# A weight sum's low part moved from VectorE to ScalarE and an accumulating DMA in an FFN up projection

## The chip, the cores and the metric

The kernel runs on one core of one Trainium2 chip, as one program with one launch. The metric is the time of the execution on the device in microseconds (us). Engines are named as in the profile: PE is TensorE's matmul, PEld its weight load, DVE is VectorE, ACT is ScalarE, POOL is GpSimd, SP is SyncE, which here only issues DMAs.

## The reference

The program is a two-layer trunk in float32 over 512 positions and 1024 channels. Each layer normalises, mixes the tokens (layer 0 by pooling and a short convolution, layer 1 by gated linear attention), adds the result to `x`, and then runs a feed-forward block, which is where the change lies:

```python
D_MODEL = 1024; SEQ = 512; DEPTH = 2; D_FF = 2816

def conv_ffn(h, w_up, conv_w, conv_b, w_down):
    u, v = jnp.split(h @ w_up, 2, axis=-1)
    u = causal_dwconv(u, conv_w, conv_b)
    return (jax.nn.gelu(u, approximate=False) * v) @ w_down

def reference(...):
    for l in range(DEPTH):
        ...
        x = x + conv_ffn(rmsnorm(x, ffn_norm[l]), ffn_w_up[l], ffn_conv_w[l], ffn_conv_b[l], ffn_w_down[l])
    return rmsnorm(x, final_norm)
```

`h @ w_up` is 512 by 1024 times 1024 by 5632 in each layer.

## The kernel before

**Two parts of every operand.** Each float32 operand is split into a high part (a copy rounded to the matmul's float32r format, written by ACT) and a low part (operand minus high part, written by DVE). A product is then three passes: weight high by data high, weight high by data low, weight low by data high.

**Pairs.** The 5632 columns of `w_up` are taken as 22 pairs, numbered here from 0 as in the code (`seven(j, base)`); a pair holds 128 columns of `v` and 128 of `u`. A pair is done with seven block products instead of eight (p1 to p7), after Strassen and Winograd. Each is three passes of four matmuls of 128x256 and is one `UNIT` (1.364 us) of the plan, so a pair is 7 units, 9.55 us. The products p1 and p2 use the left half `a1` of the pair's weights, p6 uses `s2`, p5 and p7 use the sum `s31`, p3 and p4 use the last combination `a2`. They are not done in one block: p4 and p3 of a pair come 9 and 11 units after its start, between the products of the next pair (`PE_AT`). So from a pair's start ("base") PE does p1, p2, p4 of the pair before, p6, p3 of the pair before, p5, p7. In pair 0 the order is p1, p2, p3, p6, p5 (`PE_AT_FIRST`), and the products p2 and p3 there run the weight's low pass before the data's low pass (`low_last`).

**The weights of a pair** (`seven_weights`). SP loads the block that both halves of `s31` share (`load_sum`, line 462, 512 KB into three rotating buffers). GpSimd adds the other two blocks of `w_up` onto it by an accumulating DMA (`add_sum`, line 466, 512 KB). SP loads the left half (`load_left`, line 470, 512 KB) and the right half (`load_right`, line 474, 256 KB) into three rotating `raw` buffers. ACT and DVE make high and low parts (lines 484 and 490) of `a1`, `s31`, `s2` and `a2`; DVE forms `s2` and `a2` (lines 495, 501). A high and a low part of 128x1024 lie in four rotating buffers each (`wsp`).

**The rest of a pair.** ACT copies partial results out of PSUM (`keep`, line 645, tiles `kk`, `k`, `k3`; line 679, `u`), DVE combines them (657, 660, 682), the convolution is one ACT and two DVE steps (356, 359), gelu is on ACT (627).

**The order of work.** Each step is recorded with a planned time (`at`), sorted by it, and issued in that order on PE, DVE and ACT (`run_plan`, `manual_schedule`), which so keep an order written out by hand. SP's and GpSimd's queues are ordered by the scheduler. Each engine and each queue works strictly in its order: what waits holds up all that stands behind it. In the plan the high part of `s31` is due at base - 2.7, its low part at base + 1.5. The `lead` argument gives pairs 0 to 5 a later `a2` (high at base + 2.2, low at + 4.4, instead of + 0.4 and + 3.3).

Of the kernel before, what the change touches and what calls it, by code (L numbers as in the profile page):

```python
# [10 lines left out]
AF = mybir.ActivationFunctionType  # L11
ALU = mybir.AluOpType
# [29 lines left out]
UNIT = 1.364  # L42
# [13 lines left out]
DOWN_K = (7, 7)  # L56
DOWN_AT = (0, 7)
NDOWN = 6

COLS = {}  # L60
_n = 0
# [12 lines left out]
def trunk_kernel(ctx, tc, xT, cols, w_ab, w_pool, w_abo, w_vg, w_qk, w_r, w_g2, w_go, w_up, w_dn, w_ds, outT):  # L74
    nc = tc.nc
    V, S, G, PE = nc.vector, nc.scalar, nc.gpsimd, nc.tensor
# [9 lines left out]
    def slot(dt=F32, name="s"):  # L86
        return big.tile([P, T], dt, tag="s", name=name)
# [14 lines left out]
    def half(name):  # L102
        return hp.tile([P, H], F32, tag="h", name=name)
# [15 lines left out]
    lead = []  # L119
# [53 lines left out]
    def f32(ap):  # L173
        return ap.bitcast(F32)
# [189 lines left out]
    def conv3(u, wname, bname, j, nj):  # L364
        tap = conv_steps(u, wname, bname, j, nj)
        return [tap(i) for i in range(3)][0]
# [63 lines left out]
    def at(t, fn):  # L430
        events.append((t, len(events), fn))
# [21 lines left out]
        at(t_high, lambda: steps[0]())  # L453
        at(t_low, lambda: steps[1]())

    def seven_weights(src, base, pool, sums, behind=False, lead=None, later=0.0):
        w = {}

        def load_sum():
            s31 = w["s31"] = stage[pool].tile([P, WBLK], F32, tag="sum", name="s31", bufs=sums)  # L460
            part = src[:, None, D : D + QUARTER].broadcast_to([P, 2, QUARTER])
            nc.sync.dma_start(s31.rearrange("p (a n) -> p a n", a=2), part)

        def add_sum():
            part = src.rearrange("p (a n) -> p a n", a=4)[:, 0:4:3, :]
            G.dma_start(w["s31"].rearrange("p (a n) -> p a n", a=2), part, accum_op=ALU.add)  # L466

        def load_left():
            w["raw", 0] = wp.tile([P, WBLK], F32, tag="raw", name="raw")
            nc.sync.dma_start(w["raw", 0], src[:, :D])  # L470

        def load_right():
            w["raw", 1] = wp.tile([P, WBLK], F32, tag="raw", name="raw")
            nc.sync.dma_start(w["raw", 1][:, QUARTER:], src[:, D + QUARTER :])

        def tiles(kind, wide):
            if wide:
                return wsp.tile([P, WPITCH], F32R, tag=kind, name=kind)[:, SKEW : SKEW + WBLK]
            tag, bufs = "s" + kind[0], 2 if pool == "up" else 1
            return stage[pool].tile([P, T + 64], F32R, tag=tag, name=tag, bufs=bufs)[:, SKEW : SKEW + T]  # L480

        def high(name, src, wide=True):
            h = tiles("hi", wide)
            S.activation(h, src(), AF.Copy)  # L484
            w[name] = (h, src)

        def low(name, wide=True):
            h, src = w[name]
            lo = tiles("lo", wide)
            V.tensor_tensor(lo, src(), f32(h), ALU.subtract)  # L490
            w[name] = (h, lo)

        def s2_sum():
            s2 = w["raw", 1][:, :QUARTER]
            V.scalar_tensor_tensor(
                s2, w["s31"][:, QUARTER:], -1.0, w["raw", 0][:, :QUARTER], ALU.mult, ALU.subtract
            )

        def s4_sum():
            s2 = w["raw", 1][:, :QUARTER]  # L500
            V.tensor_tensor(s2, w["raw", 0][:, QUARTER:], s2, ALU.subtract)

        def queued_sum():
            with tc.issue_after(loads[-1]):
                load_sum()

        at(base - 26.0, queued_sum if behind else load_sum)
        at(base - 20.0, add_sum)
        steps = (
            (lambda: high("a1", lambda: w["raw", 0])), (lambda: low("a1")), (lambda: high("s31p", lambda: w["s31"])),  # L510
            s2_sum, (lambda: high("s2", lambda: w["raw", 1][:, :QUARTER], False)), (lambda: low("s2", False)),
            s4_sum, (lambda: high("a2", lambda: w["raw", 1])), (lambda: low("s31p")), (lambda: low("a2")),
        )
        when = (-6.75, -4.35, -2.7, -2.4, -1.65, -0.95, -0.3, 1.55, 1.5, 3.3)
        if pool == "up":
            when = (*when[:7], *((2.2, 1.5, 4.4) if lead is not None else (0.4, 1.5, 3.3)))
        if pool == "gla":
            when = (*when[:7], 4.4, 1.5, 5.3)
        if lead is not None and lead < 2:
            when = ((-9.5, -7.6, 2.6, -8.3, -7.0, -6.0, -5.3, -4.5, 4.3, -2.6), (-3.9, -1.9, -1.2, -2.4, -1.65, -0.95, -0.3, 2.4, 1.5, 4.6))[lead]  # L520
        at(base - (18.0 if lead == 0 else 15.4), load_left)
        at(base - (13.0 if lead == 0 else 9.7), load_right)
        for n, (t, step) in enumerate(zip(when, steps)):
            at(base + t + ((0, 0, 1.2, 1.2, 0.6, 0.6)[lead or 0] if 3 <= n <= 6 else later if n == 0 else 0.0), step)

        return w
# [89 lines left out]
    def ffn(l, acc, mixed, finish, ahead, halves_last=False):  # L616
# [17 lines left out]

        def seven(j, base):
            b, q = {}, {}
            w = seven_weights(w_up[l, j], base, "up", 3, j <= 3, j if j < 6 else None, 0.8 if j in (6, 7) else 0.0)

            def product(*args):
                if not rhs:  # L640
                    rhs.update(operands(mixed))
                seven_product(w, b, rhs, *args)

            def keep(dst):
                S.activation(dst, b["x"][:, :H], AF.Copy)  # L645

            def keep_p1():
                q["k"] = slot(name="kk")
                keep(q["k"][:, lo_t])

            def keep_p7():
                q["k3"] = half("k3")
                keep(q["k3"])

            def u_high():
                q["u"] = slot(name="u")
                V.scalar_tensor_tensor(q["u"][:, hi_t], b["yz"][:, hi_t], -1.0, q["k3"], ALU.mult, ALU.subtract)

            def u_scaled():
                V.tensor_tensor(q["u"], q["u"], rs, ALU.mult)  # L660

            for name, out, first, ts in (
                ("p1", "x", True, lo_t), ("p2", "yz", True, lo_t), ("p6", "x", False, lo_t), ("p5", "yz", False, hi_t),
                ("p7", "x", False, lo_t), ("p4", "x", False, lo_t), ("p3", "yz", False, hi_t),
            ):
                apart = j in (0, NF - 1)
                if apart and name == "p3":
                    out, first = "w", True
                when = PE_AT_FIRST if j == 0 else PE_AT_LAST if j == NF - 1 else PE_AT
                t = base + when[name] * UNIT + (NORM if j == 0 and when[name] > 4 else 0.0)  # L670
                for i in range(3) if j == 0 and name == "p2" else (None,):
                    at(t + (i or 0) * UNIT / 3, lambda a=(name, out, first, ts, i, j == 0 and name in ("p2", "p3")): product(*a))
            late = UNIT + NORM if j == 0 else 0.0
            at(base + 1.45, keep_p1)
            at(base + (5.1 if j == 0 else 5.5 if j < 6 else 6.05), lambda: keep(q["k"][:, hi_t]))
            at(base + (9.0 if j == 2 else 8.25 if 2 < j < 6 else 9.55) + late, keep_p7)
            at(base + 9.95 + late, u_high)
            after = base + PAIR + (NORM + 1.6 if j == 0 else NORM + 0.5 if j == 1 else 0.0)
            at(after + 4.1, lambda: S.activation(q["u"][:, lo_t], b["x"][:, :H], AF.Copy, scale=-1.0))
            at(after + 4.5, u_scaled)  # L680
            conv_at(j, after, q)
            at(after + 10.4, lambda: V.tensor_tensor(q["k"], b["yz"], q["k"], ALU.add))
            if apart:
                hi_k = lambda: q["k"][:, hi_t]
                at(after + 10.5, lambda: V.tensor_tensor(hi_k(), b["w"][:, hi_t], hi_k(), ALU.add))
            at(after + 12.3, lambda: V.tensor_tensor(q["a"], q["k"], q["a"], ALU.mult))
# [3 lines left out]
        def split_m():  # L690
            j = len(mh)
            pool = stage["dn"] if j < NDOWN // 2 else big
            mh.append(pool.tile([P, T], F32R, tag="s", name="mh"))
# [52 lines left out]
        base = 5 * UNIT  # L746
# [3 lines left out]
        base -= PAIR  # L750
        at(base + 5.6, lambda: open_stage("dn", NDOWN))
        for t in (5.8, 6.6, 8.0, 10.3, 10.9, 11.5, 12.2, 14.5, 15.2, 16.4, 17.6, 18.3, 19.0, 20.6):
# [4 lines left out]
        o, late, ops = {}, {}, {}  # L757
# [75 lines left out]
        t = base + 9 * UNIT  # L833
# [70 lines left out]
    with tc.manual_schedule(engines=set(planned)):  # L904
        raw, hi, lo = lead[0]
# [75 lines left out]
    for j in range(4):  # L981
# [5 lines left out]
        a = conv3(c, "sc_w", "sc_b", j, 4)  # L987
# [281 lines left out]
    t = 0.0  # L1269
# [15 lines left out]
    first = True  # L1285
# [153 lines left out]
    late = t + 2.5  # L1439
# [152 lines left out]
```

## Time and profile before

| | |
|---|---|
| median of 3 runs | 1006.32 us (1005.56 to 1007.13) |
| profiled execution | 1006.93 us, of which the span is 1005.2 us |
| mean granted TensorE clock | 0.997 |
| PE busy | 994.8 us (99%) |
| DVE busy | 851.2 us (85%) |
| ACT busy | 615.8 us (61%) |
| POOL busy | 81.3 us (8%) |
| DMA, queue of SP (q1) | 117.46 MB, 37.8% of 16 engines' span |
| DMA, queue of GpSimd (q0) | 31.99 MB, 19.2% of 16 engines' span |

A row of the timeline gives start, length, engine, line, operation, what is written from what, the shape and a count; the brackets at its end give the idle time of the engine before it and what ended that. The kernel has stages: the input projection and mixer of layer 0 to about 140.6 us of the span, the up projection of layer 0 to 352, its down projection to about 475, the attention of layer 1, its up projection from about 668 to 879, and the last down projection. PE's busy share says little by itself, since matmuls are pipelined; what the kernel loses is seen where the starts of its groups of four matmuls lie further apart than elsewhere.

### The profile page before, as it was taken

The page shows a single profiled execution, that of the slowest core. Times are in us where ns is not written, and L with a number is a line of the kernel's source. Part 1 is how long each engine was busy: PE and PEld are TensorE (multiplying, and loading weights), DVE is VectorE, ACT ScalarE, POOL GpSimd, SP SyncE. Part 2 cuts the span into 40 slices and gives each one's busy share as a digit, 9 for nine tenths or more (in the row PEclk, how much of TensorE's full clock was granted, in tenths as well). Part 3 has the DMA queues.
Part 4 walks back from the last instruction along what each step waited for, and adds up shares of the span by engine and source line. Part 5 has one row for each costly group of instructions (what it writes and reads, how often), then busy time and mean ns, then how long its engine had stood idle before and what let it go on. Part 6 is the DMA issues. An engine that isn't in the chain of part 4 may idle for free.

```text
span 1005.2 us, 17757 instructions
## 1 busy us (share of the span) xinstructions
PE 994.8 (99%) x7070; PEld 927.9 (92%) x7070; DVE 851.2 (85%) x1241; ACT 615.8 (61%) x959; POOL 81.3 (8%) x105
## 2 busy tenths in 40 slices
PE   9999999999999999999999999999999999999996
PEld 7888889999999988899999998889999999988896
DVE  7886689999999997768768788889999999997775
ACT  6442467666766764445785677667766666754451
POOL 0000111111101000002000000111101101000000
PEclk9999999999999999999999999999999999999998
DMA  6523757787687454527326122676788777454522
GB/s 224 156 97 105 181 123 185 193 210 191 190 208 181 129 134 132 140 85 198 108 76 145 53 67 93 185 171 165 213 207 194 195 202 188 127 128 142 129 86 84
DMA packets 64083, 151.22 MB, mean 150 GB/s; under 512 B 5408, under 2 KB 8352, under 8 KB 64000
## 3 DMA queue, kind: packets, MB, share of 16 engines
q1 hardware_dynamic: 46640, 117.46, 37.8%
q0 software_dynamic: 16672, 31.99, 19.2%
q8 instruction: 55, 0.90, 0.3%
q10 hardware_dynamic: 688, 0.65, 0.2%
q14 instruction: 28, 0.23, 0.1%
HBM read 145.35 MB, written 2.10 MB: 147 GB/s over the span
## 4 chain that ended last, share of the span: by engine, by line
PE 91%; DVE 4%; DMA 2%; ACT 1%; issue 1%; DVEq 0%; ACTq 0%
PE stx L538 27%; PE styz L538 16%; PE dn L268 15%; PE r L1323 4%; PE abo L268 4%; PE go L268 4%; PE pc L268 2%; PE dn L538 2%; PE px L268 2%; PE pb L268 2%; DMA raw<-in_w_up 2%; PE stz L538 2%; PE vg L1111 1%; PE vg L1113 1%; PE vg L1112 1%; PE pu L268 1%
## 5 line engine op out<-in xcount | busy, mean ns | idle before, releaser
L490 DVE TENSOR_TENSOR lo<-raw,hi 128x1024 fp32r<-128x1024 f32 x112 | 136.7, 1221 | 14.1 <-ACT hi L484 13.8
L484 ACT ACTIVATE hi<-raw 128x1024 fp32r<-128x1024 f32 x112 | 117.8, 1057 | 33.2 <-DMA raw<-in_w_up 12.8
L227 DVE TENSOR_TENSOR lo<-raw,hi 128x1024 fp32r<-128x1024 f32 (+3 forms) x79 | 91.1, 1155 | 18.2 <-ACT hi L223 17.7
L466 POOL DMA_DIRECT2D s<-in_w_up x44 | 53.1, 1206 | 530.1 <-ACT yh L177 97.3
L223 ACT ACTIVATE hi<-raw 128x1024 fp32r<-128x1024 f32 (+3 forms) x79 | 78.7, 997 | 13.2 <-DMA raw<-in_w_ab 4.7
L359 DVE SCALAR_TENSOR_TENSOR cacc<-u,colt,cacc 128x511 f32<-128x511 f32 x96 | 71.5, 745 | 3.9 <-ACT cacc L356 3.8
L356 ACT ACTIVATE cacc<-u,colt 128x512 f32<-128x512 f32 x48 | 39.2, 817 | 49.5 <-DVE u L660 39.9
L490 DVE TENSOR_TENSOR lo<-s,hi 128x1024 fp32r<-128x1024 f32 x56 | 68.2, 1217 | 0.0
L538 PE MATMUL stx<-th,hi 128*128 128x256 f32 x384 | 59.4, 277 | 0.3 <-ACT kk L645 0.3
L484 ACT ACTIVATE hi<-s 128x1024 fp32r<-128x1024 f32 x56 | 59.0, 1053 | 0.7
L538 PE MATMUL stx<-th,lo 128*128 128x256 f32 x384 | 59.1, 276 | 0.0
L538 PE MATMUL stx<-tl,hi 128*128 128x256 f32 x384 | 59.1, 276 | 0.0
L538 PE MATMUL styz<-xl,hi 128*128 128x256 f32 x368 | 57.2, 277 | 0.3
L538 PE MATMUL styz<-xh,hi 128*128 128x256 f32 x368 | 56.9, 277 | 0.0
L538 PE MATMUL styz<-xh,lo 128*128 128x256 f32 x368 | 56.7, 276 | 0.0
L268 PE MATMUL dn<-mh,hi 128*128 128x512 f32 (+1 forms) x238 | 56.5, 377 | 0.0
L268 PE MATMUL dn<-mh,lo 128*128 128x512 f32 (+1 forms) x238 | 56.4, 376 | 0.0
L268 PE MATMUL dn<-ml,hi 128*128 128x512 f32 (+1 forms) x238 | 56.4, 376 | 0.0
L538 PEld LDWEIGHTS stx<-th,hi 128*128 128x128 f32 x384 | 50.7, 188 | 0.7 <-ACT kk L645 0.7
L538 PEld LDWEIGHTS stx<-tl,hi 128*128 128x128 f32 x384 | 50.7, 188 | 0.0
L538 PEld LDWEIGHTS stx<-th,lo 128*128 128x128 f32 x384 | 50.7, 188 | 0.0
L268 PEld LDWEIGHTS dn<-ml,hi 128*128 128x128 f32 x238 | 42.9, 188 | 8.2
(334 smaller groups left out, 2583.3 us busy)
## 6 DMA issues: line engine op xcount, KB each, us to landing
s<-in_w_up SPq DMA_DIRECT2D x44, 512.0 KB, 6.9
s<-in_w_up POOLq DMA_DIRECT2D x44, 512.0 KB, 7.3
raw<-in_w_up SPq DMA_DIRECT2D x44, 512.0 KB, 6.7
raw<-in_w_dn SPq DMA_DIRECT2D x32, 448.0 KB, 3.4
raw<-in_w_up SPq DMA_DIRECT2D x44, 256.0 KB, 3.6
raw<-in_w_ab SPq DMA_DIRECT2D x14, 512.0 KB, 3.6
raw<-in_w_abo SPq DMA_DIRECT2D x8, 512.0 KB, 3.6
s<-in_w_ds SPq DMA_DIRECT2D x8, 512.0 KB, 6.9
```

The source lines that it names most:

```text
L223: S.activation(parts[0], raw, AF.Copy)
L227: V.tensor_tensor(parts[1], raw, f32(parts[0]), ALU.subtract)
L268: PE.matmul(out, w[:, k, :], a[k], start=first and i == 0 and k == 0, stop=last and i == 2 and k == n - 1, skip_group_check=loose,)
L356: S.activation(acc[0], u, AF.Identity, bias=col(bname, j), scale=col(wname, 2 * nj + j))
L359: V.scalar_tensor_tensor(a, u[:, : T - i], col(wname, (2 - i) * nj + j), a, ALU.mult, ALU.add)
L466: G.dma_start(w["s31"].rearrange("p (a n) -> p a n", a=2), part, accum_op=ALU.add)
L484: S.activation(h, src(), AF.Copy)
L490: V.tensor_tensor(lo, src(), f32(h), ALU.subtract)
L538: PE.matmul(b[out][:, ts], wt[:, ks[k]], a[k], start=first and i == 0 and k == 0, stop=i == 2 and k == HK - 1, skip_group_check=True,)
L1111: PE.matmul(o[c][:, :n], xh[kk][:, cs], h[:, k, :], start=kk == 0, stop=False)
L1112: PE.matmul(o[c][:, :n], xl[kk][:, cs], h[:, k, :], start=False, stop=False)
L1323: PE.matmul(o, w[:, k, :], a[k], start=i == 0 and k == 0, stop=k == KD - 1 and i == 5, skip_group_check=True)
```

## The change

In the pairs 2 to 9 (`QUEUED`, both layers) the low part of `s31` is no longer made by DVE. ACT makes the high part at base - 3.7 instead of - 2.7, then at base - 2.6 writes minus the high part into the low part's buffer, and GpSimd issues a DMA from `s31` (SBUF) onto that buffer (SBUF) that adds. On GpSimd's queue the next `add_sum` is kept behind that DMA. The later `a2` of `lead` holds for pairs 0 to 3 only, and the delay of 0.8 (`later`) moves from the pairs 6 and 7 to pair 2. In pair 0 the third pass of p2 is moved behind the second pass of p3, and p3 is recorded by pass. The copy of p7's result in pair 0 (`keep_p7`) is planned 1.25 earlier.

```diff
+QUEUED = range(2, 10)
...
-    def seven_weights(src, base, pool, sums, behind=False, lead=None, later=0.0):
+    last_queued = []
+
+    def seven_weights(src, base, pool, sums, behind=False, lead=None, later=0.0, queued=False):
...
-            G.dma_start(w["s31"].rearrange("p (a n) -> p a n", a=2), part, accum_op=ALU.add)
+            with tc.issue_after(last_queued[-1]) if last_queued else ExitStack():
+                G.dma_start(w["s31"].rearrange("p (a n) -> p a n", a=2), part, accum_op=ALU.add)
+            last_queued.clear()
...
+        def queued_low(name):
+            h, src = w[name]
+            lo = tiles("lo", True)
+            S.activation(lo, f32(h), AF.Copy, scale=-1.0)
+            last_queued.append(G.dma_start(lo, src(), accum_op=ALU.add).ins)
+            w[name] = (h, lo)
...
-            s4_sum, (lambda: high("a2", lambda: w["raw", 1])), (lambda: low("s31p")), (lambda: low("a2")),
+            s4_sum, (lambda: high("a2", lambda: w["raw", 1])), (lambda: (queued_low if queued else low)("s31p")), (lambda: low("a2")),
...
+        if queued:
+            when = (*when[:2], -3.7, *when[3:8], -2.6, when[9])
...
-            w = seven_weights(w_up[l, j], base, "up", 3, j <= 3, j if j < 6 else None, 0.8 if j in (6, 7) else 0.0)
+            w = seven_weights(w_up[l, j], base, "up", 3, j <= 3, j if j < 4 else None, 0.8 if j == 2 else 0.0, j in QUEUED)
...
-                for i in range(3) if j == 0 and name == "p2" else (None,):
-                    at(t + (i or 0) * UNIT / 3, lambda a=(name, out, first, ts, i, j == 0 and name in ("p2", "p3")): product(*a))
+                for i in range(3) if j == 0 and name in ("p2", "p3") else (None,):
+                    wait = 1.5 * UNIT if (name, i) == ("p2", 2) else (i or 0) * UNIT / 3
+                    at(t + wait, lambda a=(name, out, first, ts, i, j == 0 and name in ("p2", "p3")): product(*a))
...
-            at(base + (9.0 if j == 2 else 8.25 if 2 < j < 6 else 9.55) + late, keep_p7)
+            at(base + (8.3 if j == 0 else 9.0 if j == 2 else 8.25 if 2 < j < 6 else 9.55) + late, keep_p7)
```

In the built program this takes 16 subtractions of 128x1024 off DVE's order and adds 16 copies of 128x1024 to ACT's and 16 DMAs to GpSimd's. On SP's queue one row moves in each layer: the right half of pair 4 now stands behind the `load_sum` of pair 6. From pair 6 on, ACT has the high part of the next pair's `s31` ahead of the copy `kk` of p6's result.

## The prediction

> **What bounds the kernel.** The page comes first: PE, DVE and the shares of the chain that ended last.
>
> ```profile
> span 1005.2 us, 17757 instructions
> ...
> PE 994.8 (99%) x7070; PEld 927.9 (92%) x7070; DVE 851.2 (85%) x1241; ACT 615.8 (61%) x959; POOL 81.3 (8%) x105
> ...
> PE 91%; DVE 4%; DMA 2%; ACT 1%; issue 1%; DVEq 0%; ACTq 0%
> ```
>
> PE sets the end: 91% of the chain is its issue, which the change leaves as it is. So the most that can be won is what PE loses in the two up stages. The timeline of PE, read at the starts of its groups of four, shows it; an undisturbed group starts 0.46 us before the next (143.89 to 144.35).
>
> ```profile
> 143.02 1.03 PE L538 MATMUL styz<-xl,hi 128*128 128x256 f32 x4
> 143.89 0.62 PE L538 MATMUL stw<-xh,hi 128*128 128x256 f32 x4
> 144.35 0.62 PE L538 MATMUL stw<-xh,lo 128*128 128x256 f32 x4
> ...
> 203.79 0.62 PE L538 MATMUL styz<-th,lo 128*128 128x256 f32 x4
> 204.66 0.73 PE L538 MATMUL stx<-th,hi 128*128 128x256 f32 x4 [0.26 <-ACT kk L645]
> ...
> 670.44 1.02 PE L538 MATMUL styz<-xl,hi 128*128 128x256 f32 x4
> 671.30 0.62 PE L538 MATMUL stw<-xh,hi 128*128 128x256 f32 x4
> ...
> 740.71 0.62 PE L538 MATMUL styz<-th,lo 128*128 128x256 f32 x4
> 741.40 0.73 PE L538 MATMUL stx<-th,hi 128*128 128x256 f32 x4
> ```
>
> Four places lose time: 0.87 - 0.46 = 0.41 us (p2's third pass, layer 0), 0.87 - 0.46 = 0.41 (before p7 of pair 6), 0.86 - 0.46 = 0.40 and 0.69 - 0.46 = 0.23 in layer 1. Together 1.45 us, or 0.14%: the gain cannot be larger. 0.2% (2.0 us) is about what a measurement of this kernel can tell from no change.
>
> Next come busy times by stretch, for pairs 2 to 9 of layer 0 and ten pairs behind them, and the DMA queues in the same pairs of layer 0, then layer 1 (its 684.80 to 761.50).
>
> ```profile
> 158.00:234.70 76.70, 76.44 (x674) 76.24 (x673) 74.15 (x102) 53.35 (x85) 9.63 (x8) 1.00 0.82 201
> 234.70:330.00 95.30, 95.30 (x843) 95.30 (x842) 90.49 (x121) 65.91 (x100) 12.03 (x10) 1.00 0.74 191
> ```
> ```profile
> q1 hardware_dynamic: 4546, 10.77, 45.7%
> q0 software_dynamic: 2339, 4.50, 35.5%
> ```
> ```profile
> q1 hardware_dynamic: 4530, 10.59, 44.0%
> q0 software_dynamic: 2229, 4.29, 34.6%
> ```
>
> Three things run close to full: PE, DVE (74.15 of 76.70 us, the third busy column) and the DMA engines (82%). Only ACT (53.35) has room. The change takes from DVE and gives to ACT and to the DMAs.
>
> **The change, part by part.** The two kinds of instruction moved, in the same stretch:
>
> ```profile
> L490 DVE TENSOR_TENSOR lo<-s,hi 128x1024 fp32r<-128x1024 f32 x8 | 9.7, 1217 | 0.0
> ```
> ```profile
> L484 ACT ACTIVATE hi<-s 128x1024 fp32r<-128x1024 f32 x8 | 8.4, 1048 | 0.0
> L356 ACT ACTIVATE cacc<-u,colt 128x512 f32<-128x512 f32 x9 | 7.3, 816 | 8.8 <-DVE u L660 8.8
> ```
>
> DVE loses 8 x 1.22 = 9.7 us a layer and falls to about 64.4 of 76.7. ACT gains a copy of the same shape as its high parts, 8 x 1.05 = 8.4, and reaches 61.8 of 76.7. GpSimd issues eight more DMAs. None of these sums bounds a stage. What decides is where things stand.
>
> (a) Pair 0, passes in another order. The pass at 143.02 reads `xl` of the last tile, which DVE finishes at 142.87 + 0.74 = 143.61:
>
> ```profile
> 142.87 0.74 DVE L579 SCALAR_TENSOR_TENSOR xl<-xall,colt,xh 128x512 fp32r<-128x512 f32 x1
> ```
>
> Put behind two passes of p3 that read `xh` alone, it starts at 143.02 + 2 x 0.46 = 143.94, after `xl` is ready. Both losses go: -0.81. Bounds -0.81 and 0 (0 if another operand, 0.4 us earlier now, is late next; the first is the low part of p6's data).
>
> (b) The stall before p7 of pair 6. The chain of waits and ACT's timeline carry it:
>
> ```profile
> 193.25 8.10 DMA raw<-in_w_up
> ```
> ```profile
> 194.59 1.04 ACT L484 ACTIVATE hi<-s 128x1024 fp32r<-128x1024 f32 x1
> ...
> 201.44 1.07 ACT L484 ACTIVATE hi<-raw 128x1024 fp32r<-128x1024 f32 x1 [1.73 <-DMA raw<-in_w_up]
> 202.41 0.36 ACT L679 ACTIVATE u<-stx 128x256 f32<-128x256 f32 x1
> 203.53 0.82 ACT L356 ACTIVATE cacc<-u,colt 128x512 f32<-128x512 f32 x1 [0.76 <-DVE u L660]
> 204.25 0.36 ACT L645 ACTIVATE kk<-stx 128x256 f32<-128x256 f32 x1
> 204.51 1.05 ACT L484 ACTIVATE hi<-s 128x1024 fp32r<-128x1024 f32 x1
> ```
>
> The left half of pair 7 leaves at 193.25, because DVE frees its buffer late, and lands at 201.35; ACT waits for it, so `kk` ends at 204.61 and p7 waits. With 1.2 us a pair off DVE the buffer comes free earlier: -0.41 and -0.23, or -0.64. Against it, in the changed order the high part of `s31` (1.05) stands between `cacc` and `kk` from pair 6 on, so a left half that lands as late as now would cost 1.05 more at each of pairs 6, 7 and 8. Bounds -0.64 and 6 x 1.05 = +6.3; I take -0.64, since DVE's lag is what made the load late.
>
> (c) The low part by DMA. PE's rows of pair 6 give the deadline:
>
> ```profile
> 196.08 0.62 PE L538 MATMUL stx<-xh,hi 128*128 128x256 f32 x4
> ```
>
> This is the pair's base; the low pass of its p5 is the row at 203.79 above, 7.71 us on. The nearest DMAs are GpSimd's accumulating ones, `add_sum` of the same 512 KB (from HBM, these eight pairs) and the sums of squares (SBUF to SBUF, 256 KB):
>
> ```profile
> L466 POOL DMA_DIRECT2D s<-in_w_up x8: 1203/1203/1208, 158.7 to 226.3; - x8
> ...
> DMA to landing us min/median/max: 5.8/8.0/9.7
> ```
> ```profile
> L585 POOL DMA_DIRECT2D acc<-sq x6: 849/896/1415, 112.8 to 664.3; - x6
> ...
> DMA to landing us min/median/max: 3.3/5.5/12.4
> ```
>
> Issue: the buffer is free only when p3 of the pair two before has ended, at 12 units, which is base - 2.7; a copy begun then ends at base - 1.6. That is the early end. Today the high part of `s31` in pair 6 begins at 194.59, or base - 1.5, and ends at base - 0.45; a copy behind it ends at base + 0.6. That is the late end. The middle is base - 0.5. With the median landing of 8.0 the sum is ready at base + 7.5, and PE needs it at + 7.7: just in time. With 5.8 it comes at + 5.3, with 9.7 at + 9.2. So about half of the pairs come late, by up to 1.5, as a mean some 0.6 (an estimate from that spread, a little under half of its upper end, since PE's wait gives the pairs behind it time). 16 pairs x 1/2 x 0.6 = +4.8. Of the two rows I take that of `add_sum`, because the size and the pairs are the same.
>
> The bounds of (c) are 0 and what the DMA engines lack. In layer 0, 35.5% of 76.7 us is 27.2 us for 4.50 MB, so eight more of 0.524 MB take 25.4 us, 33%; 45.7 + 35.5 + 33 = 114%, or 11 us too much. In layer 1 26.5 us for 4.29 MB gives 34%, and 44.0 + 34.6 + 34 = 112.6%, or 9.7 us. Upper end +20.7. In the ten pairs behind, 0.74 leaves more room, and those are not touched.
>
> By the Trainium skill (DMA: Bandwidth & Descriptors, "Anatomy of one DMA — SWDGE (gpsimd) path") a GpSimd DMA takes about 2.0 us and its bytes over 436 GB/s; an estimate by it is 3.2 us for 512 KB, so the low part would be there by base + 3.8 even from the late issue and (c) would be 0, the first rival below. The rows of this trace stand against it: 5.8 at the least.
>
> (d) Waits added. ACT's copy waits for p3's end; behind it stand the `u`, `k3` and `sh` copies. On GpSimd the next `add_sum` stands behind the new DMA, which waits for ACT; its sum is due 15 us later, so this costs nothing unless the queue falls a whole transfer behind. SP's waits, and its rows in pair 6:
>
> ```profile
> SPq L462 <- DVE lo L490: 37.4, 19, 5.6
> ```
> ```profile
> 200.47 0.38 SPq L462 DMA_DIRECT2D s<-in_w_up  x1
> 202.18 0.33 SPq L470 DMA_DIRECT2D raw<-in_w_up  x1
> ```
>
> On SP, `load_sum` of pair j + 3 needs the buffer that the new DMA reads: released by DVE today, so that the load leaves at 200.47 (base + 4.4 of pair 6), and at about base + 7.5 then. Behind it stand the left and right half of pair j + 2. SP already waits 37.4 us at this place, 19 times. The left half moves from base + 6.1 (202.18 in pair 6) to about + 8, which by the 8.10 above lands at base + 16, 3 us before its pair: no stall by itself, but the reserve of (b) is used. The right half of pair 4, now behind the `load_sum` of pair 6, leaves some 3 us later; its first reader is the high part of `a2`, which PE needs 9 units after the base: 0.
>
> **Sum.** -0.81 (a) - 0.64 (b) + 4.8 (c) = +3.3 us. The profiled execution, 1006.93 (its span and 1.7 around it), would be 1010.2; it is 0.6 above the median of the runs, so the median goes from 1006.3 to 1009.6.
>
> **Rivals.** *The transfer is hidden.* If ACT starts its copy at base - 2.6 as planned, landings up to 9.2 us are in time, and the median of 8.0 is. For it: DVE is freed, and ACT's longest idle time, 8.8 us ahead of `cacc`, is a wait for DVE. Against: the DMA engines are at 82% before the 33% are added. It gives 1006.3 - 1.45 = 1004.8, and decides where the new DMA lands within 7.7 us of the base in every pair. *The DMA engines become the bound.* For it: the 114% above. Against: no stretch above is at full share, so what the engines still take there is not shown, and buffers are loaded some 20 us ahead, which a deficit must first use up. 1006.3 - 1.45 + 20.7 = 1025.6. *The kk copies come late,* by (b)'s order, at the three pairs of each layer while the DMAs are no faster: 1006.3 - 0.81 + 6.3 = 1011.8. *The change does not do what it says:* if GpSimd's queue held the new DMA behind an `add_sum` still waiting, each would be late by one transfer; the built order puts it ahead of that of pair j + 2, so I give this nothing.
>
> **How the numbers follow.** Chances: forecast 0.42, hidden 0.41, kk late 0.09, DMA-bound 0.08. Hidden gives 1004.8, inside 0.2%, except 0.04 for a measurement below 1004.3. So faster 0.04, same 0.37, slower 0.59. The range reaches from 1004.6 (all that can be won, and a little noise) to 1017 (half of the upper end of (c) and no gain), and leaves out 0.1 on either side. The slower cases alone, the likeliest side, lie between 1008.3 and 1017.
>
> **What would show it.** (a) right: the starts of p2's first and p3's third pass 5 x 0.46 apart, without a gap, at 142 and 669 us. (b) right: no idle time of PE before `stx` released by `kk`. (c) right: gaps of PE before the `styz<-th,lo` passes of the pairs 2 to 9, released by a DMA onto `lo`, and a median landing of that DMA near 8 us. DVE should fall by 9.7 us a layer and ACT rise by 8.4. The prediction is wrong if the new DMA lands in about 5 us, if DVE's freed time brings ACT to its planned start, or if the DMA share of pairs 2 to 9 goes to full and the stall repeats at every pair.

## The result and the profile after

The changed kernel takes 1024.82 us (median of 4 runs, 1024.14 to 1025.81), the kernel before 1006.38 in the same runs: a ratio of 1.0182, with a 95% interval from 1.0169 to 1.0194. That is 18.4 us slower; 1009.6 was forecast. The span grew from 1005.2 to 1024.1 us.

The page of the changed kernel: its head, the shares of the chain that ended last by engine, and one of the costliest groups (busy time, mean ns, then the idle time ahead of it and what ended most of that).

```profile
span 1024.1 us, 17790 instructions
...
PE 1002.1 (98%) x7070; PEld 932.5 (91%) x7070; DVE 834.4 (81%) x1225; ACT 626.2 (61%) x975; POOL 95.6 (9%) x121
...
PE 77%; DMA 11%; DVE 6%; ACT 5%; issue 2%; DVEq 0%; SPq 0%; ACTq 0%
...
L489 ACT ACTIVATE hi<-raw 128x1024 fp32r<-128x1024 f32 x112 | 118.1, 1057 | 58.4 <-DMA raw<-in_w_up 36.3
```

DVE's busy time fell by 16.8 us (19.4 forecast) and ACT's rose by 10.4 (16.8 forecast). But PE fell from 91% to 77% of the chain and DMA rose from 2% to 11%. ACT now waits 36.3 us for `raw`, the loads of the weight's halves. Before, that wait was this (us in total, times, longest):

```profile
ACT hi L484 <- DMA raw<-in_w_up: 12.8, 12, 2.1
```

The same view after, for SP's queue and for PE:

```profile
SPq L465 <- DMA lo<-s: 101.0, 16, 10.3
...
PE stx L552 <- ACT kk L659: 7.2, 6, 3.1
PE styz L552 <- DMA lo<-s: 5.0, 7, 1.2
```

All 16 new DMAs hold up `load_sum` on SP, for 101 us in all. (Not all of it is new: over the whole program the waits of `load_sum` for DVE's low part fell from 86.6 to 56.9 us.) At the end of the chain PE waits 7.2 us for the copy `kk` (0.3 before) and 5.0 us for the low part itself. Counted as distances between the starts of PE's matmuls beyond their usual ones, the up stages lost 10.5 and 9.6 us, against 1.1 and 0.9 before: 18.1 of the 18.9 us by which the span grew.

The longest stall, pair 4 of layer 0, in the timeline of SP, ACT and PE:

```profile
175.45 0.38 SPq L465 DMA_DIRECT2D s<-in_w_up  x1
175.93 0.41 SPq L479 DMA_DIRECT2D raw<-in_w_up  x1
...
180.95 0.62 PE L552 MATMUL stx<-th,lo 128*128 128x256 f32 x4
181.87 1.21 POOL L470 DMA_DIRECT2D s<-in_w_up  x1 [3.48 <-DMA s<-in_w_up]
183.28 1.06 ACT L489 ACTIVATE hi<-raw 128x1024 fp32r<-128x1024 f32 x1 [4.79 <-DMA raw<-in_w_up]
184.25 0.36 ACT L659 ACTIVATE kk<-stx 128x256 f32<-128x256 f32 x1
```

The load of pair 6's sum leaves at 175.45, when the new DMA of pair 3 has landed. The right half of pair 4 stands behind it (175.93, 4.0 us later than before). ACT needs that half for the high part of `a2` and waits 4.79 us; behind it stands `kk`, for which PE stands still, 3.1 us by the waits. The same load in the kernel before:

```profile
171.97 0.33 SPq L474 DMA_DIRECT2D raw<-in_w_up  x1
```

The windows that follow (PE's busy time and records come first; the granted clock, the DMA engines' share and GB/s last) show a second loss:

```profile
181.00:185.00 4.00, 0.90 (x7) 0.71 (x6) 0.63 (x1) 1.59 (x3) 1.21 (x1) 0.87 1.03 277
185.00:188.00 3.00, 3.00 (x15) 3.00 (x15) 2.43 (x3) 1.44 (x4) 0.00 (x0) 0.50 0.99 197
188.00:192.00 4.00, 4.00 (x26) 4.00 (x25) 2.02 (x3) 3.34 (x5) 0.21 (x1) 0.66 0.83 172
192.00:196.00 4.00, 4.00 (x38) 4.00 (x37) 3.57 (x6) 2.57 (x6) 1.89 (x2) 1.00 1.03 245
```

PE comes back at half clock: 26 matmuls in 4 us, where the next 4 us hold 38. That is (1 - 0.50) x 3 + (1 - 0.66) x 4 = 2.9 us more.

From there the same chain goes round in the later pairs. Two pairs on:

```profile
205.84 1.06 ACT L489 ACTIVATE hi<-raw 128x1024 fp32r<-128x1024 f32 x1 [0.64 <-DMA raw<-in_w_up]
...
208.42 0.38 SPq L465 DMA_DIRECT2D s<-in_w_up  x1
208.89 0.66 SPq L475 DMA_DIRECT2D raw<-in_w_up  x1
...
216.30 1.06 ACT L489 ACTIVATE hi<-raw 128x1024 fp32r<-128x1024 f32 x1 [1.53 <-DMA raw<-in_w_up]
...
227.50 1.06 ACT L489 ACTIVATE hi<-raw 128x1024 fp32r<-128x1024 f32 x1 [2.80 <-DMA raw<-in_w_up]
```

The left half leaves 0.47 us behind `load_sum`, and 7.4 us later ACT begins with it at 216.30, after a wait that grows from pair to pair (0.64, 1.53, then 2.80).

### The profile page after: what moved, and what is told of

It reads as the page before. It is cut to its first block, busy times and chain, and to the rows that moved or that the text cites. A ratio compares the mean times of both kernels' runs of the same rounds, so it can differ in the third digit from the quotient of the medians.

```text
span 1024.1 us, 17790 instructions
## 1 busy us (share of the span) xinstructions
PE 1002.1 (98%) x7070; PEld 932.5 (91%) x7070; DVE 834.4 (81%) x1225; ACT 626.2 (61%) x975; POOL 95.6 (9%) x121
## 3 DMA queue, kind: packets, MB, share of 16 engines
q0 software_dynamic: 18976, 40.38, 22.9%
## 4 chain that ended last, share of the span: by engine, by line
PE 77%; DMA 11%; DVE 6%; ACT 5%; issue 2%; DVEq 0%; SPq 0%; ACTq 0%
PE stx L552 20%; PE dn L269 15%; PE styz L552 11%; DMA raw<-in_w_up 8%; PE r L1338 4%; PE go L269 3%; PE abo L269 3%; ACT hi L489 2%; PE pc L269 2%; PE dn L552 2%; PE pb L269 2%; PE px L269 2%; DVE lo L495 2%; PE stz L552 2%; PE vg L1126 1%
## 5 line engine op out<-in xcount | busy, mean ns | idle before, releaser
L489 ACT ACTIVATE hi<-raw 128x1024 fp32r<-128x1024 f32 x112 | 118.1, 1057 | 58.4 <-DMA raw<-in_w_up 36.3
L495 DVE TENSOR_TENSOR lo<-raw,hi 128x1024 fp32r<-128x1024 f32 x112 | 136.7, 1221 | 20.0 <-ACT hi L489 19.8
L674 DVE TENSOR_TENSOR u<-u,rs 128x512 f32<-128x512 f32 x44 | 30.4, 691 | 29.1 <-ACT u L694 29.1
L495 DVE TENSOR_TENSOR sl<-raw,sh 128x512 fp32r<-128x512 f32 x56 | 38.8, 693 | 17.4 <-ACT sh L489 16.3
```

## The experiments

Three theories stood against each other. **W**: the load of the sum waits on SP for the new DMA, and the loads behind it come late. **D**: the DMA engines cannot carry the added bytes. **K**: the other changes of the plan (the shorter `lead`, the swap of pair 4's right half on SP) make the loss.

**The parts of the plan.** First pair 0's order alone, on the kernel before.

```diff
-                for i in range(3) if j == 0 and name == "p2" else (None,):
-                    at(t + (i or 0) * UNIT / 3, lambda ...)
+                for i in range(3) if j == 0 and name in ("p2", "p3") else (None,):
+                    wait = 1.5 * UNIT if (name, i) == ("p2", 2) else (i or 0) * UNIT / 3
+                    at(t + wait, lambda ...)
...
-            at(base + (9.0 if j == 2 else
+            at(base + (8.3 if j == 0 else 9.0 if j == 2 else
```

> The kernel before with only the other order of pair 0's passes (third pass of p2 behind the second pass of p3, copy of p7's result planned earlier). All theories: the gaps of 0.41 and 0.40 us go and nothing else moves, so 0.8 us less than before, 1005.5 us.

Measured: 1006.36 against 1006.89 us, ratio 0.9985 (0.9965 to 1.0004). Pair 0's gaps are gone in both layers. The size is near the -0.8 expected, but the interval holds 1.

Then all of the plan, without the DMA.

```diff
-QUEUED = range(2, 10)
+QUEUED = ()
```

> The changed kernel with an empty list of queued pairs: the new order of pair 0, the shorter lead and the moved delay stay, the low part is made by VectorE again, no new DMA and no new copy. Theory W (SP's load of the sum waits for the new DMA and holds up the loads behind it) and theory D (the DMA engines lack throughput): back to 1004.5 to 1007 us. Theory K (the high part of a2, put ahead of kk in pairs 4 and 5, causes the first stall of each layer): a stall of 2 to 4 us in pair 4 of each layer stays, 1009 to 1014 us.

Measured: 1007.67 us, ratio 1.0003 (0.9987 to 1.0018). It lies just above the range of W and D and below that of K. K falls as the cause of the 18 us: the plan alone costs one short wait for `kk` in pair 4 of each layer, which uses up what pair 0 gains. The rest needs the DMA.

```profile
PE stx L552 <- ACT kk L659: 1.3, 2, 0.6
```

**Pair 4 put back**, with the DMA in place.

```diff
-        at(base - 26.0, queued_sum if behind else load_sum)
+        def sum_behind():
+            with tc.issue_after(lefts[-2]), tc.issue_after(lefts[-1]):
+                load_sum()
+
+        at(base - 26.0, queued_sum if behind else sum_behind if kept else load_sum)
...
-            w = seven_weights(..., j if j < 4 else None, ..., j in QUEUED)
+            w = seven_weights(..., j if j < 6 else None, ..., j in QUEUED, j == 6)
```

(`lefts` collects the loads of both halves.)

> The changed kernel with the longer lead for pairs 4 and 5 again, and on SP's queue the right half of pair 4 ahead of the load of the sum of pair 6, as in the kernel before; the new DMA stays in all pairs. If the first stall of each layer (3.3 and 2.7 us) with the half clock behind it (some 3 us) is a loss of its own, 8 to 10 us come back, 1015 to 1017 us. If the waits of the later pairs only take its place, 1019 us or more.

Measured: 1026.46 us, ratio 1.0192 (1.0177 to 1.0207). Nothing comes back; the largest stall has only moved, to pair 6. PE's waits:

```profile
PE styz L557 <- DMA lo<-s: 8.1, 6, 2.6
PE stx L557 <- ACT kk L664: 6.1, 4, 3.0
```

So the first stall was where the loop showed first, not its cause.

**Traffic without a wait, and with it.** Two kernels add to the kernel before, in the same 16 pairs, an accumulating DMA of 512 KB onto a scratch buffer that nothing reads. They differ in the source, and so in the buffer that the DMA holds.

```diff
+        def extra_sum():
+            h, _ = w["s31p"]
+            ...
+            last_extra.append(G.dma_start(extra["t"], f32(h), accum_op=ALU.add).ins)
...
+        if loaded:
+            at(base - 2.65, extra_sum)
```

> The kernel before with one more accumulating DMA of 512 KB in each of the pairs 2 to 9, from the high part of the sum onto a scratch buffer that nothing reads, issued where the changed kernel issues its own; it only adds work. The sum's buffer is released by VectorE as before. Theory D: the same DMA load as the changed kernel, so 10 to 18 us more than before, 1016 to 1024 us. Theory W: no load waits longer than before, 1006 to 1010 us.

```diff
-            h, _ = w["s31p"]
-            last_extra.append(G.dma_start(extra["t"], f32(h), accum_op=ALU.add).ins)
+            s31 = w["s31"]
+            S.activation(s31[:, :16], s31[:, :16], AF.Copy)
+            last_extra.append(G.dma_start(extra["t"], s31, accum_op=ALU.add).ins)
```

> The kernel before with the extra DMA of the traffic-only kernel, but read from the weight sum itself instead of from its high part (a copy of 16 columns of the sum onto themselves by ScalarE keeps the start at the same place); it only adds work. Same bytes, same order on SP's queue; the only difference is that the sum's buffer, and so the load of the sum of pair j+3 with the loads behind it, now waits for the DMA. Theory W: 5 to 10 us more than the traffic alone, 1016 to 1021 us. If a wait at that place is harmless, as the prediction had it: 1010 to 1012 us, as the traffic alone.

Measured: 1010.90 us (1.0038, 1.0020 to 1.0055) for the traffic, 1026.83 us (1.0206, 1.0167 to 1.0245) with the hold. Pairs 2 to 9 of layer 0 in the two, as one window each, the traffic alone first:

```profile
158.00:234.70 76.70, 75.33 (x662) 74.93 (x661) 71.11 (x97) 50.74 (x82) 16.76 (x16) 1.00 1.00 243
```
```profile
158.00:234.70 76.70, 71.40 (x621) 70.55 (x621) 67.54 (x93) 49.93 (x86) 15.63 (x15) 1.00 0.98 222
```

With the traffic alone the DMA engines are full (1.00, 243 GB/s), and that costs 4.0 us, just above W's range and far below D's. The hold adds 15.9 us, more than W's 5 to 10, at a slightly lower share: same bytes, same order on SP, another buffer. What it adds in waits, first the traffic alone, then with the hold:

```profile
PE stx L553 <- ACT kk L661: 2.2, 4, 1.0
```
```profile
PE stx L554 <- ACT kk L662: 14.1, 12, 2.7
...
SPq L474 <- DMA extra<-s: 85.1, 16, 9.7
```

**The wait taken away from the changed kernel.** The first try gave the sum a fourth buffer and nothing else (and made room for it by a narrower pitch of two small tiles, as every kernel here that adds a buffer does).

```diff
-base, "up", 3, j <= 3
+base, "up", 4, j <= 3
```

> The changed kernel with four buffers for the weight sum in the up stages instead of three, so that the load of the sum of pair j+3 no longer waits for the new DMA of pair j. The bytes moved are the same. Theory W: most of the 18.4 us comes back, 1006 to 1011 us; what is left is the first stall of pair 4, because the right half of pair 4 may still stand behind a waiting load. Theory D: 1020 us or more, since the DMA engines have the same work.

Measured: 1037.71 us, ratio 1.0299 (1.0262 to 1.0336). That is outside W's range and inside D's open one (1020 or more), but it decides nothing. The scheduler used the free buffer to put each `load_sum` one pair earlier on SP's queue, where it waits as before:

```profile
SPq L465 <- DMA lo<-s: 98.8, 16, 11.0
...
PE styz L552 <- DMA lo<-s: 10.0, 5, 4.9
PE stx L552 <- ACT kk L659: 7.2, 5, 3.0
```

So the edit had not removed the wait, and here the low part came late as well. The second try keeps each `load_sum` behind the halves of the pair two before, so that the buffer it needs belongs to a DMA long landed.

```diff
-        at(base - 26.0, queued_sum if behind else load_sum)
+        at(base - 26.0, queued_sum if behind else sum_behind if kept else load_sum)
...
-            w = seven_weights(..., "up", 3, j <= 3, j if j < 4 else None, ..., j in QUEUED)
+            w = seven_weights(..., "up", 4, j <= 3, j if j < 6 else None, ..., j in QUEUED, 3 < j < 14)
```

> The changed kernel with four buffers for the sum, the load of the sum of pair j+3 kept behind the right half of pair j+1 on SP's queue, and the longer lead for pairs 4 and 5: the load then needs the buffer of pair j-1, whose DMA has long landed, so nothing on SP waits for the new DMA. The bytes are the same as in the changed kernel. Theory W: 1006 to 1011 us, since only the traffic is left, which alone cost 4 us. Theory D, or the low part itself being late at PE: 1014 us or more.

Measured: 1009.01 us, ratio 1.0028 (1.0010 to 1.0045). Some 16 of the 18.4 us are back with all 16 DMAs in place, at the same bytes, as W had it. Its waits of PE, and pairs 2 to 9:

```profile
PE stx L557 <- ACT kk L664: 2.0, 3, 0.9
PE styz L557 <- DMA lo<-s: 0.7, 2, 0.4
```
```profile
158.00:234.70 76.70, 75.39 (x651) 74.79 (x651) 63.94 (x92) 57.65 (x91) 16.85 (x16) 1.00 0.99 232
```

The low part is late by 0.7 us in all, where the changed kernel lost 5.0. The DMA engines are as full as ever (0.99). Is that the rest? Half the DMAs, in every other pair:

```diff
-QUEUED = range(2, 10)
+QUEUED = range(2, 10, 2)
```

> The kernel without the wait (four buffers, load of the sum kept behind the right half), with the new DMA in the pairs 2, 4, 6 and 8 alone; VectorE makes the low part in 3, 5, 7 and 9. Half the added bytes. If what is left in that kernel (2 to 4 us above before) is traffic that the DMA engines lack, most of it goes, since 82% and half of 33% is below full: 1005 to 1007 us. If it is the low part's own lateness, half stays: 1007.5 to 1009 us.

Measured: 1006.66 us, ratio 0.9998 (0.9989 to 1.0007), at a share of 0.92:

```profile
158.00:234.70 76.70, 76.70 (x679) 76.70 (x678) 71.17 (x99) 56.23 (x91) 14.51 (x13) 1.00 0.92 221
```

The remainder goes when half of the bytes go, as the traffic reading had it. This kernel also has half of the copies on ACT and of the late low parts; but the traffic alone, without either, cost 4.0 us.

**The wait without traffic.** Two kernels put a DMA of 16 columns of the sum on GpSimd's queue. In these, and in the next two, the loads on SP are kept in the order of the kernel before.

```diff
+            S.activation(s31[:, :16], s31[:, :16], AF.Copy)
+            last_extra.append(G.dma_start(extra["t"], s31[:, :16], accum_op=ALU.add).ins)
...
+            at(base + 5.6, extra_sum)
```

> The kernel before with a DMA of 16 columns of the sum, started by a ScalarE copy planned at base + 5.6, in each of the pairs 2 to 9; it only adds work, and next to no bytes. It releases the sum's buffer at about base + 8, as late as the changed kernel does. Theory W: the wait alone costs 3 to 8 us, 1010 to 1015 us. Theory D: 1006 to 1007.5 us, because no traffic is added.

```diff
-            at(base + 5.6, extra_sum)
+            at(base + 2.5, extra_sum)
```

> As the kernel that only holds the sum's buffer, but with the ScalarE copy that starts the small DMA planned at base + 2.5 instead of + 5.6. The longer hold delayed the load of the sum by 6 us a pair and cost 53 us in 16 pairs, 3.3 a pair, so about 2.9 us of delay were covered. Theory W with that reserve: this hold delays the load by some 3 us and costs 0 to 10 us, 1007 to 1017 us. If the loss does not depend on how long the buffer is held, but on what the added ScalarE copy and GpSimd's waits do: again more than 1040 us.

Measured: 1059.98 us (1.0525, 1.0507 to 1.0543) and 1057.10 us (1.0498, 1.0483 to 1.0512). Both miss, and the second shows that the place of the copy hardly matters. GpSimd's and SP's rows of the second tell why:

```profile
187.14 1.43 POOL L470 DMA_DIRECT2D extra<-s  x1
192.36 0.38 SPq L475 DMA_DIRECT2D s<-in_w_up  x1
198.66 1.20 POOL L480 DMA_DIRECT2D s<-in_w_up  x1 [10.09 <-DMA s<-in_w_up]
199.37 1.43 POOL L470 DMA_DIRECT2D extra<-s  x1
```

The small DMA releases a load; the `add_sum` that needs this load waits on GpSimd; and the next small DMA stands behind it. The loop takes 199.37 - 187.14 = 12.2 us a pair, where PE needs 9.5. These two measured a loop of their own, not the one in question. Two more kernels issue the small DMA on ACT's own queue, which adds nothing to GpSimd.

```diff
+            nc.scalar.dma_start(extra["t"], w["s31"][:, :16])
...
+            at(base + 1.0, extra_sum)
```

> The kernel before with a DMA of 16 columns of the sum (8 KB) started on ScalarE's queue at base + 1.0 of the plan in the pairs 2 to 9, ahead of the copy kk; it only adds work. No bytes to speak of, nothing added to GpSimd. The load of the sum should leave at about base + 6 instead of base + 4.4. If 3 us of reserve are there, as the prediction had it: 1006 to 1008 us. If every delay costs: 1.6 us a pair less what ScalarE's idle time covers, 1012 us or more.

```diff
-            at(base + 1.0, extra_sum)
+            at(base + 3.0, extra_sum)
```

> As the kernel with the short hold on ScalarE's queue, but the DMA starts at base + 3.0 of the plan, behind the high part of the next pair's a1. The load of the sum should leave at about base + 9, some 4.5 us later than before. Theory W: beyond the reserve of 3 us the delay costs about 1.5 us a pair or more, 1015 to 1030 us, with ScalarE waiting for the left half. Theory D (the loss needs the added traffic): 1006 to 1008 us.

Measured: 1007.43 us (1.0005, 0.9995 to 1.0014) and 1037.92 us (1.0300, 1.0273 to 1.0327), the second above W's range. Pairs 2 to 9 of layer 0 in the one with the longer hold:

```profile
158.00:247.00 89.00, 80.77 (x672) 79.59 (x671) 72.77 (x100) 51.90 (x83) 9.63 (x8) 0.96 0.72 163
```

The DMA engines idle more than in the kernel before (0.72 against 0.82), and still 31 us are lost. So a loss of this size needs no full DMA engines; a late release is enough. But the two kernels differ by more than a length. In the second the small DMA (`extra`) stands on ACT right behind the high part of the next pair's left half, and starts when that has got its load:

```profile
187.22 1.06 ACT L494 ACTIVATE hi<-raw 128x1024 fp32r<-128x1024 f32 x1 [4.40 <-DMA raw<-in_w_up]
187.25 0.47 ACTq L466 DMA_DIRECT2D extra<-s  x1
```

So the release waits for a left half, and the next left half waits behind the load that this release lets go. That is again a loop of the kernel's own: its 31 us are not the price of a delay of fixed length, and the point at which a delay begins to cost was not measured. The short hold shows only that a release about 1 us later was free.

**Which load carries it.** The changed kernel with the left half ahead of the waiting `load_sum`, in pairs 4 to 12 (`sum_last` is `load_sum` kept behind the last two loads recorded).

```diff
-        at(base - 26.0, queued_sum if behind else load_sum)
+        at(base - (24.5 if last else 26.0), queued_sum if behind else sum_last if last else load_sum)
```

> The changed kernel with another order on SP's queue in the pairs 4 to 12: the left half of pair j+2 goes ahead of the load of the sum of pair j+3, which still waits for the new DMA of pair j; the right half stays behind it. If the late left half, which ScalarE waits for, carries the loss: 12 us or more come back, 1006 to 1013 us. If the right half or the sum itself is what comes late: 1018 us or more.

Measured: 1016.71 us, ratio 1.0119 (1.0071 to 1.0167), with runs from 1014.4 to 1028.4; the profile is of the longest, so its numbers are upper ends. (In it, from pair 7 of layer 1 on, each pair takes 10.08 us instead of 9.52 at a granted clock of 1.00; no run shows why.) The time lies between the two forecasts: somewhat under half of the loss is back. In its trace PE waits for `kk` nowhere in the up stages: that link is the left half's. What is left is another one:

```profile
718.30 1.21 POOL L471 DMA_DIRECT2D s<-in_w_up  x1 [7.80 <-DVE cacc L360]
719.02 1.42 POOL L503 DMA_DIRECT2D lo<-s  x1
...
732.12 1.22 PE L559 MATMUL styz<-th,lo 128*128 128x256 f32 x4 [4.12 <-DMA lo<-s]
```

Now the sum itself is loaded later. The load that the `add_sum` at 718.30 needs landed at 717.71 (the brackets name DVE, whose signal came last), so this `add_sum` and a new DMA leave 0.72 us apart. The new one lands 13.1 us later, at 732.08 (median of the 16: 7.2), and the low part comes late.

**A version that beats both?** The new order of pair 0, four buffers with the loads' order kept, no new DMA: the no-wait kernel with

```diff
-QUEUED = range(2, 10)
+QUEUED = ()
...
-0.8 if j == 2 else 0.0
+0.8 if j in (6, 7) else 0.0
```

> The kernel before with the new order of pair 0's passes and four buffers for the sum, the load of the sum kept behind the right half of the pair two before; no new DMA, VectorE makes all low parts. It is the candidate to beat both. All theories: pair 0's gaps of 0.8 us go, and with loads that leave earlier the gaps of 0.64 us ahead of p7 may go too: 0.8 to 1.45 us less than before, 1005 to 1006 us.

Measured: 1006.61 against 1006.75 us, ratio 0.9994 (0.9985 to 1.0003). PE's excess in the up stages falls to 0.4 us in each layer, but the time cannot be told from the kernel before. It misses the 1005 to 1006 expected, and no version here is measurably faster than the kernel before.

## Why the prediction was wrong

**The step that failed is (d), which put the added wait on SP at no cost.** It named the wait, its place and its size: `load_sum` would leave at about base + 7.5. Measured over pairs 2 to 9 of layer 0: base + 7.5 on average (from 4.6 to 10.6). It also named the loads behind. What was wrong is the deadline: the left half "lands at base + 16, 3 us before its pair: no stall by itself". Its first reader is not its own pair's product. It is ACT, in order ahead of `kk`, which PE needs before p7 of the pair before. The kernel before had it in its trace: the left half of pair 7 landed at 201.35 (the rows shown under (b)), and that pair began at 206.14. The first rows of pairs 4, 5 and 7:

```profile
177.04 0.62 PE L538 MATMUL stx<-xh,hi 128*128 128x256 f32 x4
...
186.56 0.62 PE L538 MATMUL stx<-xh,hi 128*128 128x256 f32 x4
...
206.14 0.62 PE L538 MATMUL stx<-xh,hi 128*128 128x256 f32 x4
```

So a left half must land 206.14 - 201.35 = 4.8 us before its pair, and pair 6 already stood still for 0.26 us by that. The 3 us of reserve were 1.8 us too few. Put into (d)'s own numbers: 7.5 + 0.5 (the left half behind the sum) + 8.1 (its landing) + 4.8 = 20.9 us, where two pairs take 19.04 (9.52 each, 186.56 - 177.04). That is 1.9 us too long in two pairs, and 0.93 x 16 = 15 us. The hold measured 15.9 on top of the traffic, and its removal gave back some 16. That the numbers meet so closely is luck in part: 8.1 is the landing of one load. In the changed kernel the left halves left at base + 8.0 and took 7.3 on average.

The same sum for each kernel, with means over pairs 2 to 9 of layer 0 taken from the rows of SP's and PE's timelines. Estimate is 16 times half of what the sum exceeds 19.04 by. The leaving times have each kernel's own stalls in them. So the column is an accounting, not a forecast: where PE waits for the left half at every pair, the sum is simply the time that two pairs took.

| kernel | left half leaves, after its base | landing | + 4.8 | estimate, us | measured, us |
|---|---|---|---|---|---|
| before | 6.4 | 6.6 | 17.8 | 0 | - |
| short hold on ACT's queue | 6.8 | 6.8 | 18.4 | 0 | +0.5 |
| no wait | 5.1 | 8.6 | 18.5 | 0 | +2.0 |
| traffic only | 6.4 | 8.1 | 19.3 | 2 | +4.0 |
| changed | 8.0 | 7.3 | 20.1 | 8.5 | +18.4 |
| traffic and hold | 9.2 | 7.0 | 21.0 | 16 | +19.8 |
| long hold on ACT's queue | 11.3 | 6.9 | 22.9 | 31 | +31.0 |

It comes near in all but the changed one. Two kernels outside the table do not follow it: left half first (by the sum 0, measured +10.0) and four buffers alone (2, measured +30.8). In both PE waits longest for the low part (8.1 and 10.0 us).

In the changed kernel 4.8 is too little, because of a cost that (b) named and then put aside: the high part of `s31` ahead of `kk`. Behind the left half that ACT takes up at 216.30:

```profile
219.12 1.04 ACT L489 ACTIVATE hi<-s 128x1024 fp32r<-128x1024 f32 x1
220.06 0.36 ACT L659 ACTIVATE kk<-stx 128x256 f32<-128x256 f32 x1
```

This makes `kk` 0.94 us later in three of the eight pairs (`kk` of pairs 6, 7 and 8; (b) had 1.05 for each). (b) took it as harmless since the loads would come earlier; they came later. With it the sum is 20.5 on average and the estimate 11 us. Against the 18.4 measured stand besides PE's 5.0 us for the low part, 2.9 us of half clock, and the stalls of pair 4, which come by the right half (3.3 and 2.7 us). These add up to more than is left, so they overlap.

**The right half of pair 4** was costed at 0 in (d), by PE's need of `a2` nine units after the base. The same slip: ACT waited 4.79 us for it with `kk` behind, since the shorter `lead` of the change puts `a2` ahead of `kk` there. As pair 4 put back shows, mending this alone wins nothing.

**(c), the low part just in time: its numbers came out, by luck in part.** The new DMA started at base - 1.3 to + 0.3 in layer 0 (forecast - 0.5) and landed after 5.6 to 10.3 us, 8.2 in the middle (forecast 8.0). Four of layer 0's eight landed later than the 7.7 us allowed (forecast: half), and PE waited 5.0 us (forecast 4.8):

```profile
L502 POOL DMA_DIRECT2D lo<-s x16: 896/896/901, 158.1 to 769.5; - x16
...
DMA to landing us min/median/max: 5.6/8.2/10.3
```

But without the wait on SP the same DMAs landed after 6.2 us in the middle (4.6 to 8.7), 14 of 16 in time, and only 0.7 us of PE's wait stays. Most of the 5.0 us was no cost of (c)'s own, but came with the loop.

By the Trainium skill (DMA: Bandwidth & Descriptors, "Anatomy of one DMA — SWDGE (gpsimd) path") an estimate was 3.2 us; none of the changed kernel's 16 came under 5.6, and none under 4.6 without the wait. The prediction was right to take the trace's row.

**(a)** was right: the gaps of pair 0 are gone wherever its order was changed. **(b)** was right in that the stall before p7 of pair 6 is gone where nothing else is late, and wrong in its reason: it is also gone in the kernel of the plan alone, and in layer 0 of that with pair 0's order alone, where VectorE keeps all its work.

**The rivals.** *DMA engines the bound* forecast 1025.6 us, close to what came, but by a cause that measured 4.0 us. A share of 1.00 over eight pairs cost far less than the 20.7 worked out from the shares: the traffic-only kernel moved its bytes at 243 GB/s where the kernel before moved 201. The prediction's sign for it was seen all the same: a share of 0.97 in pairs 2 to 9 of layer 0 and a stall that comes back. A full share stood beside the loss and was not its cause. *The kk copies come late* named the link that PE felt, and ACT's order did add up to 0.94 us at the three pairs of each layer; but it left out the load behind the wait, which is what made the left halves late. *Hidden* was wrong for the same reason as (d).

What stays open: how the changed kernel's 18.4 us divide between the left halves, the right half of pair 4, ACT's order and the low part; they feed each other, and no run took them apart.

## What to carry to other kernels

When a change lets a slow operation hold a buffer longer, follow the load that refills it through its queue: count what stands behind it, and take as deadline not the pair that uses the data but the first instruction that waits for it in order, with all that stands behind that one on its engine. Add up the loop (release, queue, landing, work to the next release) and compare it with the time of the pairs that it spans; below that time a delay is free (here 6.8 us after the base instead of 6.4), above it the excess, shared among the pairs spanned (here two), is paid at every pair. Check too whether what releases the buffer itself waits for a load behind it: then the loop is shorter and the loss larger. Another buffer helped here only where the queue's order was kept as well.

## What the runs showed of the hardware

A stall of PE cost more than its length in some places and not in others. In the changed kernel 3.1 us of waiting halved the clock (0.50, shown above). In layer 1 this wait left the clock at 1.00:

```profile
720.43 0.73 PE L552 MATMUL stx<-th,sh 128*128 128x256 f32 x4 [2.49 <-ACT kk L659]
```

With the longer hold on ACT's queue a shorter one halved it, as the window behind it shows:

```profile
200.62 1.11 PE L550 MATMUL stx<-th,hi 128*128 128x256 f32 x4 [1.92 <-ACT kk L658]
```
```profile
201.00:204.00 3.00, 3.00 (x16) 3.00 (x16) 3.00 (x5) 2.31 (x4) 0.00 (x0) 0.50 1.03 199
```

The Trainium skill (TensorE: Matmul & The Clock Gate, "Why this matters for your kernels") advises to leave no idle gaps of TensorE above some 3 us; the first stall agrees, the last one shows that 1.9 us can be enough. The length alone did not decide it here: 1.92 us halved the clock, 2.49 us did not. So a stall of about 2 us may cost more than its length, up to the 2.9 us seen behind the longest one; what else decides stays open.
